# A two-layer decoder step on one core: the feed-forward input products of 18 of 22 column blocks as seven block products instead of eight

## The chip, the cores and the metric

The kernel runs on one core of a Trainium2 chip. The metric is the device time of one execution in microseconds (us). Engines are named as in the profile: PE is TensorE (its weight loads stand apart as PEld), DVE is VectorE, ACT is ScalarE, POOL is GpSimd, SP is SyncE, which here only issues transfers.

## The reference, cut to what matters

1,024 prompt tokens and 8 single new tokens go through two layers, an HGRN2 recurrence and a latent attention, each with a gated feed-forward behind it. Only the feed-forward is touched:

```
def swiglu(h, w_in, w_out):
    g, u = jnp.split(h @ w_in, 2, axis=-1)
    return (jax.nn.silu(g) * u) @ w_out
...
x = x + rmsnorm(mix, g[1])
x = x + rmsnorm(swiglu(rmsnorm(x, g[2]), w_ffn_in[l], w_ffn_out[l]), g[3])
```

The width is 1,024, w_in has 2 x 2,816 columns, and everything is float32.

## The kernel before, in words

All 1,032 tokens lie on the free axis, in three sets s of W = 344, and the model width is 8 chunks of 128 partitions. A float32 product is made of three fp32r products (`mm3`, lines 177 to 179): high weight by high x, high weight by low x, low weight by high x. `k.xh[s]` and `k.xl[s]` hold the high and the low half of x of a set, before the normalisation: the factor r[s] of the RMS norm is multiplied in after the product.

`ffn` walks the 2,816 hidden columns in 22 blocks f of 128. A block has a gate product and an up product for each set, each with 8 chunks of the width: 2 x 3 x 8 x 3 = 144 matmuls of 128 x 344. DVE multiplies the product by r[s] (L552, L556), ACT takes the silu (L553), POOL multiplies gate and up (L557), ACT and DVE split the result u into gh and gl (L129, L130), which stay in SBUF. One block behind follows the output product: 3 sets x 8 chunks x 3 = 72 matmuls of 128 x 344 (`out_chunk`), which DVE adds to acc (L582). The last three blocks' output products are made together, set by set, in the finishing stage (`outf`).

`k.weight` loads 512 KB of weights into a `raw` buffer (two of them, L148, on SP's queue), ACT casts the high half (L151), and POOL subtracts for the low half (L155). Weight tiles `w` have three buffers.

`finish` is what stands between two phases: for each set the sum of squares of the result (32-column matmuls of L252), its RMS norm, the residual x_d read back from DRAM, the new x, its two halves (L221, L222), and the squares of the new x (L252 again, or L198 for the last set, whose r is formed later). While the last set goes through this, PE has four products of the next phase to make, of the sets 0 and 1 (`first`).

The program is put in order per engine by a scheduler when it is built; an engine takes its instructions strictly in that order. PSUM has eight banks, all in one pool.

Of the kernel before, what the change touches and what calls it, by code (L numbers as in the profile page):

```python
# [23 lines left out]
NS = 3  # L24
W = T // NS
FF = 2816
# [11 lines left out]
class Core:  # L38
# [123 lines left out]
    def open_pre(self):  # L162

        self.pre, pool = self.right("pre", 2)
        return pool

    def close_pre(self):
        if self.pre is not None:
            self.pre.close()
            self.pre = None  # L170

    def mm3(self, out, terms, first=True, last=True):

        nc = self.nc
        n = len(terms)
        for i, ((wh, wl), (ah, al)) in enumerate(terms):
            nc.tensor.matmul(out, lhsT=wh, rhs=ah, start=first and i == 0, stop=False)  # L177
            nc.tensor.matmul(out, lhsT=wh, rhs=al, start=False, stop=False)  # L178
            nc.tensor.matmul(out, lhsT=wl, rhs=ah, start=False, stop=last and i == n - 1)  # L179
# [116 lines left out]
def finish(k, pool, outf, acc, g_post, g_next, x_d, prefetch, at, kn):  # L296
    first, lags = kn['first'], kn['lags']

# [14 lines left out]
    def norm(s, sq):  # L313
        last = s == NS - 1
        for _ in range(lags[0]):
            yield
        r1 = yield from sq.rstd()
        s2 = Squares(k, pool, rev=kn['rev2'])
        ss = []
        for c in range(KC):  # L320
            y = acc[s][:, c, :]
            xs = pool.tile([P, W], F32, name="xs", tag="xs", bufs=6)
# [3 lines left out]
            k.put_x(s, c, y, g_next)  # L326
            if not last:
# [11 lines left out]
        if not last:  # L339
            for _ in range(lags[1]):  # L340
                yield
            rs[s] = yield from s2.rstd(k.new_r(s))
        else:
            rs[s] = lambda pool, tags: result(k.rstd(pool, ss, k.one, D, k.new_r(s), tags))
# [9 lines left out]
    for s in range(NS):  # L354
        for i, sq in enumerate(products(s)):
            if s == at and i == 0:
                prefetch()
            catch_up(kn['rate'] if i else kn['rate0'])
        behind.append(norm(s, sq))
    for i, m in enumerate(first):  # L360
# [163 lines left out]
LAST = 3  # L524


def ffn_first(w_in):

    w_in = w_in.rearrange("(c p) f -> p c f", p=P)
    return [(w_in[:, :, :P], KC, P), (w_in[:, :, FF:FF + P], KC, P)]  # L530


def ffn(k, w_in, w_out, r, end):
    nc, tc = k.nc, k.tc
    w_in = w_in.rearrange("(c p) f -> p c f", p=P)
    with ExitStack() as st:
        accp = st.enter_context(tc.tile_pool(name="accp", bufs=1, reuse_waits="tile"))
        acc = [k.new_acc() if k.accs is not None and s < NS - 1 else accp.tile([P, KC, W], F32, name=f"acc{s}") for s in range(NS)]
        gp = st.enter_context(tc.tile_pool(name="gp", bufs=2, reuse_waits="tile"))
        G = {}  # L540
        wo = {}

        def inp(f):

            wg = k.weight(w_in[:, :, f * P:(f + 1) * P], KC, P)
            wu = k.weight(w_in[:, :, FF + f * P:FF + (f + 1) * P], KC, P)
            for s in range(NS):
                if callable(r[s]):
                    r[s] = r[s](gp, ("u", "a", "u"))
                pg = k.xproduct(wg, s, 0)  # L550
                a = gp.tile([P, W], F32, name="a")
                nc.vector.tensor_tensor(out=a, in0=pg, in1=r[s], op=ALU.mult)  # L552
                nc.scalar.activation(out=a, in_=a, func=AF.Silu)  # L553
                pu = k.xproduct(wu, s, 1)
                u = gp.tile([P, W], F32, name="u")
                nc.vector.tensor_tensor(out=u, in0=pu, in1=r[s], op=ALU.mult)  # L556
                nc.gpsimd.tensor_tensor(out=u, in0=u, in1=a, op=ALU.mult)  # L557
                gh = gp.tile([P, W], F32R, name="gh", bufs=NS * LAST + 1)
                gl = gp.tile([P, W], F32R, name="gl", bufs=NS * LAST + 1)
                k.split(gh, gl, u)  # L560
                G[f, s] = (gh, gl)
                if s == 0:
                    wo[f] = k.weight(w_out[f * P:(f + 1) * P, :].unsqueeze(1), 1, D, None, gp if f < NF - 1 else None)
                yield

        units = [inp(f) for f in range(NF)]
        for f, n in ((0, NS - 1), (1, NS - 1), (0, 1)):
            for _ in range(n):
                next(units[f])
        for f in range(1, NF):  # L570
            if f < NF - 1:
                for _ in units[f]:
                    pass
            k.close_pre()
            if f <= NF - LAST:
                for s in range(NS):
                    for dc in range(KC):
                        po = out_chunk(k, wo, G, [f - 1], s, dc)
                        if f == 1:
                            nc.scalar.copy(acc[s][:, dc, :], po)  # L580
                        else:
                            nc.vector.tensor_tensor(out=acc[s][:, dc, :], in0=po, in1=acc[s][:, dc, :], op=ALU.add)  # L582

        def outf(s, dc):
            if dc == 0:
                next(units[NF - 1])
# [1190 lines left out]
def tile_yoco_step(ctx, tc, a, c, o, phases=("hgrn", "ffn0", "mla", "ffn1")):  # L1777
# [16 lines left out]
    firsts = {  # L1794
        "hgrn": lambda: hgrn_first(a["w_in_a"][0]),
        "ffn0": lambda: ffn_first(a["w_ffn_in"][0]),
        "mla": lambda: mla_first(a, cols[:, 64:72]),
        "ffn1": lambda: ffn_first(a["w_ffn_in"][1]),
    }
    k.prefetch(firsts[phases[0]]())  # L1800
    load = lambda *tiles: load_x(k, a["x_prompt"], a["x_sample"], pre[phases[0]], x_d, *tiles)
    if phases[0] != "hgrn":
        with tc.tile_pool(name="ld", bufs=2, reuse_waits="tile") as lp:
            r = [g() for g in load(lambda: lp.tile([P, D], F32, name="xt"), lambda: lp.tile([P, KC, W], F32, name="y0"), lp)]
    for n, ph in enumerate(phases):
# [4 lines left out]
        def end(st, outf, acc):  # L1810
            prefetch, at = None, 1
            if ph in ("hgrn", "mla") and nxt is not None:
                prefetch = lambda: k.prefetch(firsts[nxt](), k.open_pre())
# [5 lines left out]
            return finish(k, fp, outf, acc, gain(l, gi + 1), pre[nxt], x_d, prefetch, at, KN[ph])  # L1819
# [19 lines left out]
        else:  # L1839
            r = ffn(k, a["w_ffn_in"][l], a["w_ffn_out"][l], r, end)  # L1840
# [69 lines left out]
```

## Time and profile before

| | |
|---|---|
| time, median of 3 runs | 2927.92 us (2924.86 to 2930.66) |
| profiled execution | 2927.77 us, span 2926.0 us, mean granted TensorE clock 0.977 |
| PE busy, share of the span | 2790.2 us, 95% |
| DVE, ACT, POOL busy | 1718.8, 1129.5, 999.3 us |
| moved by DMA | 242.51 MB, mean 83 GB/s |

The HGRN2 phase takes the first 640 us or so, the first feed-forward lies at about 750 to 1550 us, the attention up to about 2150 us, and the second feed-forward after that. [...]

### The profile page before, as it was taken

The page shows a single profiled execution, that of the slowest core. Times are in us where ns is not written, and L with a number is a line of the kernel's source. Part 1 is how long each engine was busy: PE and PEld are TensorE (multiplying, and loading weights), DVE is VectorE, ACT ScalarE, POOL GpSimd, SP SyncE. Part 2 cuts the span into 40 slices and gives each one's busy share as a digit, 9 for nine tenths or more (in the row PEclk, how much of TensorE's full clock was granted, in tenths as well). Part 3 has the DMA queues.
Part 4 walks back from the last instruction along what each step waited for, and adds up shares of the span by engine and source line. Part 5 has one row for each costly group of instructions (what it writes and reads, how often), then busy time and mean ns, then how long its engine had stood idle before and what let it go on. Part 6 is the DMA issues. An engine that isn't in the chain of part 4 may idle for free.

```text
span 2926.0 us, 54566 instructions
## 1 busy us (share of the span) xinstructions
PE 2790.2 (95%) x22360; PEld 2623.6 (90%) x22360; DVE 1718.8 (59%) x3298; ACT 1129.5 (39%) x2422; POOL 999.3 (34%) x912
## 2 busy tenths in 40 slices
PE   7998988889999999999999999979999999999998
PEld 7988888878899999999978899846889999999998
DVE  7888888863444444444358888794363444444435
ACT  7666666655511111111255766523453111111112
POOL 3555555552432233332332111242153332223320
PEclk9999999989999999999999999989999999999999
DMA  5122222152311111111132112486431111111112
GB/s 184 54 67 67 67 67 65 60 191 99 117 48 50 44 44 51 46 49 51 37 100 83 46 48 69 169 346 223 133 107 51 47 48 51 44 44 49 46 61 92
DMA packets 230970, 242.51 MB, mean 83 GB/s; under 512 B 19074, under 2 KB 211120, under 8 KB 224704
## 3 DMA queue, kind: packets, MB, share of 16 engines
q1 hardware_dynamic: 205456, 170.14, 19.0%
q0 software_dynamic: 7456, 43.00, 4.0%
q10 hardware_dynamic: 17808, 25.89, 2.5%
q8 instruction: 176, 2.88, 0.4%
q14 instruction: 74, 0.61, 0.1%
HBM read 194.87 MB, written 44.12 MB: 82 GB/s over the span
## 4 chain that ended last, share of the span: by engine, by line
PE 83%; DVE 9%; ACT 4%; issue 2%; DMA 1%; POOL 1%; SPq 0%; DVEq 0%; ACTq 0%; POOLq 0%
PE ps L177 24%; PE ps L178 24%; PE ps L179 23%; PE ps L252 2%; DVE E L873 1%; DVE turned L1458 1%; PE ps L1385 1%; PE ps L1458 1%; DVE X L877 1%; PE ps L903 1%; PE ps L940 1%; ACT E L875 1%; DVE X L1008 1%; PE ps L198 1%; DVE oy L1010 1%
## 5 line engine op out<-in xcount | busy, mean ns | idle before, releaser
L177 PE MATMUL ps<-xh,w 128*128 128x344 f32 x3360 | 1103.8, 329 | 1.9 <-ACT xh L221 1.9
L178 PE MATMUL ps<-xl,w 128*128 128x344 f32 x3360 | 1083.5, 323 | 1.6 <-DVE xl L222 1.6
L179 PE MATMUL ps<-xh,w 128*128 128x344 f32 x3360 | 1078.7, 322 | 0.0
L155 POOL TENSOR_TENSOR w<-raw,w 128x512 fp32r<-128x512 f32 (+1 forms) x360 | 466.3, 1316 | 809.5 <-ACT w L151 803.0
L177 PEld LDWEIGHTS ps<-xh,w 128*128 128x128 f32 x3360 | 638.6, 190 | 24.7 <-issue 12.1
L178 PEld LDWEIGHTS ps<-xl,w 128*128 128x128 f32 x3360 | 638.5, 190 | 15.3 <-issue 8.3
L179 PEld LDWEIGHTS ps<-xh,w 128*128 128x128 f32 x3360 | 637.5, 190 | 5.7 <-issue 5.6
L582 DVE TENSOR_TENSOR acc<-ps,acc 128x344 f32<-128x344 f32 x864 | 397.4, 513 | 0.0
L151 ACT CAST w<-raw 128x1024 fp32r<-128x1024 f32 (+4 forms) x206 | 206.5, 1004 | 423.7 <-PE ps L179 324.0
L177 PE MATMUL ps<-gh,w 128*128 128x344 f32 x1056 | 338.6, 323 | 0.5 <-ACT gh L129 0.3
L179 PE MATMUL ps<-gh,w 128*128 128x344 f32 x1056 | 338.5, 321 | 0.0
L178 PE MATMUL ps<-gl,w 128*128 128x344 f32 x1056 | 338.0, 320 | 0.0
L557 POOL TENSOR_TENSOR u<-u,a 128x344 f32<-128x344 f32 x132 | 122.1, 926 | 533.6 <-DVE u L556 529.0
L556 DVE TENSOR_TENSOR u<-ps,r 128x344 f32<-128x344 f32 x132 | 68.1, 516 | 388.6 <-PE ps L179 388.4
L129 ACT CAST gh<-u 128x344 fp32r<-128x344 f32 x132 | 63.5, 481 | 504.3 <-POOL u L557 504.3
L552 DVE TENSOR_TENSOR a<-ps,r 128x344 f32<-128x344 f32 x132 | 68.1, 516 | 231.6 <-PE ps L179 225.5
L177 PEld LDWEIGHTS ps<-gh,w 128*128 128x128 f32 x1056 | 198.2, 188 | 5.3 <-issue 1.7
L179 PEld LDWEIGHTS ps<-gh,w 128*128 128x128 f32 x1056 | 198.6, 188 | 1.1 <-issue 1.1
L178 PEld LDWEIGHTS ps<-gl,w 128*128 128x128 f32 x1056 | 198.6, 188 | 1.1 <-DVE gl L130 0.8
L130 DVE TENSOR_TENSOR gl<-u,gh 128x344 fp32r<-128x344 f32 x132 | 70.1, 531 | 150.9 <-ACT gh L129 150.9
L553 ACT ACTIVATE a<-a 128x344 f32<-128x344 f32 x132 | 64.5, 490 | 224.0 <-DVE a L552 223.8
L876 POOL TENSOR_TENSOR X<-lin,E 128x256 f32<-128x256 f32 x112 | 115.8, 1040 | 88.9 <-ACT E L875 32.4
(375 smaller groups left out, 4047.0 us busy)
## 6 DMA issues: line engine op xcount, KB each, us to landing
raw<-in_w_ffn_in_dram SPq DMA_DIRECT2D x88, 512.0 KB
raw<-in_w_ffn_out_dram SPq DMA_DIRECT2D x44, 512.0 KB
raw<-in_w_in_a_dram SPq DMA_DIRECT2D x32, 512.0 KB
xs<-x_d SPq DMA_DIRECT2D x72, 172.0 KB
x_d<-acc ACTq DMA_DIRECT2D x9, 1376.0 KB
x_d<-y SPq DMA_DIRECT2D x3, 1376.0 KB
od_a<-oh ACTq DMA_DIRECT2D x24, 172.0 KB
od_a<-ol ACTq DMA_DIRECT2D x24, 172.0 KB
```

The costliest lines, as they stand in the source:

```text
L130: (lo_eng or self.nc.vector).tensor_tensor(out=lo, in0=src, in1=hi, op=ALU.subtract)
L151: nc.scalar.copy(wh[:, :n], raw[:, :n])
L155: eng.tensor_tensor(out=wl[:, sl], in0=raw[:, sl], in1=wh[:, sl], op=ALU.subtract)
L177: nc.tensor.matmul(out, lhsT=wh, rhs=ah, start=first and i == 0, stop=False)
L178: nc.tensor.matmul(out, lhsT=wh, rhs=al, start=False, stop=False)
L179: nc.tensor.matmul(out, lhsT=wl, rhs=ah, start=False, stop=last and i == n - 1)
L552: nc.vector.tensor_tensor(out=a, in0=pg, in1=r[s], op=ALU.mult)
L553: nc.scalar.activation(out=a, in_=a, func=AF.Silu)
L556: nc.vector.tensor_tensor(out=u, in0=pu, in1=r[s], op=ALU.mult)
L557: nc.gpsimd.tensor_tensor(out=u, in0=u, in1=a, op=ALU.mult)
L582: nc.vector.tensor_tensor(out=acc[s][:, dc, :], in0=po, in1=acc[s][:, dc, :], op=ALU.add)
L876: nc.gpsimd.tensor_tensor(out=Xl[:, :, 0, :], in0=kl[:, :, 0, :], in1=El[:, :, 0, :], op=ALU.mult)
```

## The change: what it does

Both feed-forwards are rebuilt.

- **x normalised.** `finish` with `gated` forms r for all three sets, multiplies the new x by its gain and by r, and splits that (8 more DVE products, ACT copies and subtractions a set). The squares of set 2 go through the 32-column matmuls as well (L256 now). The buffers `xs` go from 6 to 4.
- **Plain blocks.** Blocks 0 to 3 stay 144 matmuls of 344 columns (`plain`). Blocks 0 and 1 of the sets 0 and 1 are made inside `finish` (`before`): eight products instead of four.
- **Seven products.** For blocks 4 to 21 gate and up are seen as a 2 x 2 block product: rows gate and up, inner halves of the width, columns two sets of tokens. The 1,032 tokens are four sets of Q = 258 (the fourth is gathered from the three ends of 86), taken as two pairs. Each pair needs seven products of 4 chunks (`PRODUCTS`), with combined weights S1 to S4 (`make`: POOL forms them, ACT and DVE split them, seven parts of 128 x 512 a block) and combined tokens T1 to T4 (`tokens`, `last_tokens`, once per layer). A block is then 2 x 7 x 4 x 3 = 168 matmuls of 128 x 258 (`visit`), and the sums are taken by accumulating further products on the same PSUM bank and by ACT and DVE outside it.
- **Through DRAM.** The split silu(g) u of each block is stored to `g_d` and read back (1,032 KB a block) in a separate output stage: block 0 alone, then nine pairs, then the last three in `outf` as before.

```
+Q = T // 4
+R = W - Q
...
 def finish(...):
+            if not gated:
+                k.put_x(s, c, y, g_next)
+            if not last or gated:
                 s2.add(acc[s][:, c:c + 1, :], None, xs)
...
+            r = rs[s] = yield from s2.rstd(k.new_r(s))
+            for c in range(KC if gated else 0):
+                xs = pool.tile([P, W], F32, name="xs", tag="xs", bufs=4)
+                nc.vector.scalar_tensor_tensor(out=xs, in0=acc[s][:, c, :], scalar=g_next[:, c:c + 1], in1=r, op0=ALU.mult, op1=ALU.mult)
+                k.split(k.xh[s][:, c, :], k.xl[s][:, c, :], xs, nc.gpsimd if last and c % 2 else None)
...
+    if gated:
+        for _ in gated.before():
+            catch_up(3)
...
+PRODUCTS = (("A11", "B11"), ("S1", "T1"), ("S2", "T2"), ("S4", "B22"), ("S3", "T3"), ("A12", "B21"), ("A22", "T4"))
...
+    def make(self, f):
+        A = []
+        for i in range(2):
+            raw = k.wp.tile([P, 1024], F32, name="raw", tag="raw", bufs=2)
+            nc.sync.dma_start(out=raw.rearrange("p (a b) -> p a b", a=KC), in_=self.columns(f, i))
+            A += [raw[:, :512], raw[:, 512:]]
+        src = dict(zip(("A11", "A12", "A21", "A22"), A))
+        how = {"S1": ("A21", "A22", ALU.add), "S2": ("S1", "A11", ALU.subtract), "S4": ("A12", "S2", ALU.subtract), "S3": ("A11", "A21", ALU.subtract)}
+        for name, _ in PRODUCTS:
+            if name in how:
...
+                nc.gpsimd.tensor_tensor(out=src[name], in0=src[a], in1=src[b], op=op)
+            w = self.slot()
+            hi, lo = w[:, :512], w[:, 512:1024]
+            k.split(hi, lo, src[name])
...
+    def visit(self, f):
...
+        for name, xname in PRODUCTS:
+            wh, wl = self.parts.pop((f, name))
+            for p in range(2):
+                xh, xl = self.X[p, xname]
...
+                k.mm3(to, [((wh[:, j, :], wl[:, j, :]), (xh[:, j, :], xl[:, j, :])) for j in range(KH)], not more, True, more)
+                if name == "A11":
+                    nc.scalar.copy(t1[p], to)
+                elif name == "S1":
+                    nc.scalar.copy(t5[p], to)
+                elif name == "S2":
+                    nc.scalar.copy(t2[p], to)
+                elif name == "S4":
+                    nc.vector.tensor_tensor(out=t2[p], in0=to, in1=t2[p], op=ALU.add)
+                    nc.scalar.activation(out=t2[p], in_=t2[p], func=AF.Silu)
+                elif name == "S3":
+                    nc.vector.tensor_tensor(out=t5[p], in0=to, in1=t5[p], op=ALU.add)
+                    nc.gpsimd.tensor_tensor(out=t5[p], in0=t5[p], in1=t2[p], op=ALU.mult)
+                    store(2 * p + 1, self.pool.tile([P, 2, Q], F32R, name="gs", tag="td"[p]), t5[p])
+                elif name == "A12":
+                    nc.vector.tensor_tensor(out=t1[p], in0=to, in1=t1[p], op=ALU.add)
+                    nc.scalar.activation(out=t1[p], in_=t1[p], func=AF.Silu)
+                else:
+                    nc.vector.tensor_tensor(out=t1[p], in0=to, in1=t1[p], op=ALU.mult)
...
 def ffn(...):
+    def fetch(f, new, pool=None):
+            t = new([P, 2, T])
+            nc.sync.dma_start(out=t.bitcast(F32), in_=g_d[f])
...
+            wo[f] = k.weight(w_out[f * P:(f + 1) * P, :].unsqueeze(1), 1, D, None, pool)
...
+        while f < NF - LAST:
+            fs = range(f, min(f + (GROUP if f else 1), NF - LAST))
+            for s in range(NS):
+                for dc in range(KC):
+                    n = fs[-1] + 1 + s
+                    if dc == 0 and s < 2 and n < NF:
+                        fetch(n, lambda shape: gp.tile(shape, F32R, name="G", bufs=4), gp if n % 2 else None)
+                    po = out_chunk(k, wo, G, fs, s, dc)
+                    if f == 0:
+                        nc.scalar.copy(acc[s][:, dc, :], po)
+                    else:
+                        nc.vector.tensor_tensor(out=acc[s][:, dc, :], in0=po, in1=acc[s][:, dc, :], op=ALU.add)
```

Three places of the built order follow, each before the change and after it where both have one.

On ACT, in the middle of a feed-forward, with the buffers' numbers: `w` are weight halves being cast, `a` and `gh` the gate and the split result. Before:

```order
L151 CAST w_11837<-raw_11836 128x1024
L151 CAST w_11591<-raw_11590 128x1024
L553 ACTIVATE a_11555<-a_11555 128x344
L129 CAST gh_11586<-u_11583 128x344
L553 ACTIVATE a_11621<-a_11621 128x344
L129 CAST gh_11652<-u_11649 128x344
L151 CAST w_11843<-raw_11842 128x1024
```

After, from the second product of a visit to its fifth (`t5` and `t2` are temporaries of the pairs 0 and 1, `S` the combined weights, `gs` the split result):

```order
L724 COPY t50_10487<-ps_10474 128x258
L724 COPY t51_10502<-ps_10489 128x258
L727 COPY t20_10518<-ps_10441 128x258
L727 COPY t21_10532<-ps_10456 128x258
L131 CAST w_10538<-raw_10534 128x512
L131 CAST w_10538<-S_10569 128x512
L730 ACTIVATE t20_10518<-t20_10518 128x258
L730 ACTIVATE t21_10532<-t21_10532 128x258
L131 CAST gs_10587<-t50_10487 128x258
L131 CAST w_10613<-S_10611 128x512
L131 CAST w_10613<-S_10646 128x512
```

ACT now empties PSUM, casts parts for the next block, and issues the stores, all in one line; a cast that waits for a transfer or for POOL stands ahead of the silus.

On ACT, where the first layer's last visit ends and the output stage begins (`acc` are the sums of the output product), after the change; the place is new:

```order
L131 CAST gs<-t_13919 128x258
L703 DMA g_d<-gs 256x1x258
L131 CAST gs<-t_13934 128x258
L703 DMA g_d<-gs 256x1x258
L153 CAST w<-raw 128x1024
L809 COPY acc_14144<-ps 128x344 x8
L153 CAST w<-raw 128x1024
L809 COPY acc_14145<-ps 128x344 x8
```

The first cast of w writes where gs lay (it waits for the store of the row above it), and the eight copies that free the PSUM banks stand behind it.

On SP's queue, in the second feed-forward: `xs<-x_d` are the three residuals for the kernel's last stage. Before, they stand behind all weights:

```order
L148 DMA raw<-in_w_ffn_in_dram 128x8x128 x2
L148 DMA raw<-in_w_ffn_out_dram 128x1024
L512 DMA xs<-x_d 128x2752 x3
L502 DMA out_dram<-yt 128x1024 x2
L502 DMA out_dram<-yt 88x1024
```

After:

```order
L616 DMA raw<-in_w_ffn_in_dram 128x8x128 x36
L150 DMA raw<-in_w_ffn_out_dram 128x1024 x3
L527 DMA xs<-x_d 128x2752 x3
L150 DMA raw<-in_w_ffn_out_dram 128x1024
L475 DMA g_row<-in_norm_gains_dram 128x1024
L785 DMA G<-g_d 128x2064 x4
L150 DMA raw<-in_w_ffn_out_dram 128x1024 x4
```

They moved to the end of the visits, where x is no longer needed, and ahead of the first reads of g_d.

## Rows read from the trace of the kernel before

**Rows 1.** The page: busy time and share of engines; PE in 40 slices; the chain.

```profile
PE 2790.2 (95%) x22360; PEld 2623.6 (90%) x22360; DVE 1718.8 (59%) x3298; ACT 1129.5 (39%) x2422; POOL 999.3 (34%) x912
...
PE   7998988889999999999999999979999999999998
...
PE ps L177 24%; PE ps L178 24%; PE ps L179 23%; PE ps L252 2%; DVE E L873 1%; DVE turned L1458 1%; PE ps L1385 1%; PE ps L1458 1%; DVE X L877 1%; PE ps L903 1%; PE ps L940 1%; ACT E L875 1%; DVE X L1008 1%; PE ps L198 1%; DVE oy L1010 1%
```

**Rows 2.** Windows: length, busy (instructions) of PE, PEld, DVE, ACT, POOL; clock, DMA, GB/s.

```profile
1000.00:1050.00 50.00, 50.00 (x321) 50.00 (x320) 25.07 (x55) 8.56 (x12) 15.47 (x13) 1.00 0.19 53
1050.00:1100.00 50.00, 50.00 (x320) 50.00 (x319) 19.62 (x43) 8.85 (x14) 15.64 (x14) 1.00 0.11 34
```

**Rows 3.** Timeline of PE: 24 matmuls of 256 columns lie between the two rows.

```profile
1619.05 0.28 PE L177 MATMUL ps<-w,ch 128*128 128x256 f32 x1
...
1621.89 0.28 PE L177 MATMUL ps<-w,ch 128*128 128x256 f32 x1
```

**Rows 4.** By tile, ch: duration min/median/max; first and last start; the same matmuls.

```profile
L177 PEld LDWEIGHTS ps<-w,ch x64: 187/188/191, 1618.9 to 1828.9; 128*128 128x128 f32 x64
```

**Rows 5.** Windows at the entries of the two feed-forwards, columns as in 2.

```profile
760.00:770.00 10.00, 7.62 (x49) 7.33 (x47) 10.00 (x11) 6.36 (x13) 9.10 (x8) 1.00 0.35 144
770.00:780.00 10.00, 5.91 (x20) 5.00 (x21) 7.09 (x14) 5.59 (x9) 6.11 (x6) 0.66 0.34 98
...
2160.00:2170.00 10.00, 9.77 (x63) 9.49 (x61) 10.00 (x11) 6.69 (x15) 8.64 (x8) 1.00 0.39 142
2170.00:2180.00 10.00, 3.70 (x9) 2.79 (x10) 7.42 (x12) 5.18 (x6) 5.99 (x5) 0.74 0.27 88
2180.00:2190.00 10.00, 10.00 (x61) 10.00 (x60) 4.31 (x8) 3.40 (x8) 6.18 (x8) 0.92 0.50 159
```

**Rows 6.** Timeline of PE around a 32-column reduction (L252), and at the entry wait.

```profile
1516.56 0.32 PE L178 MATMUL ps<-xl,w 128*128 128x344 f32 x1
1516.81 0.77 PE L252 MATMUL ps<-xs,one 128*32 128x344 f32 x2
1517.50 0.42 PE L179 MATMUL ps<-xh,w 128*128 128x344 f32 x1
1517.76 0.32 PE L177 MATMUL ps<-xh,w 128*128 128x344 f32 x1
...
774.09 2.63 PE L198 MATMUL ps<-ss,one 128*128 128x344 f32 x4 [6.48 <-DVE a L552]
```

**Rows 7.** By tile, raw: duration min/median/max of the weight cast and its subtractions.

```profile
L155 POOL TENSOR_TENSOR w<-raw,w x360: 726/1291/1800, 13.8 to 2842.6; 128x512 fp32r<-128x512 f32 x176, 128x256 fp32r<-128x256 f32 x4
L151 ACT CAST w<-raw x206: 405/1048/1292, 12.6 to 2839.8; 128x1024 fp32r<-128x1024 f32 x93, 128x256 fp32r<-128x256 f32 x4, 128x768 fp32r<-128x768 f32 x2, 128x512 fp32r<-128x512 f32 x2
...
L155 DVE TENSOR_TENSOR w<-raw,w x36: 417/684/2389, 651.0 to 2059.1; 128x512 fp32r<-128x512 f32 x28, 128x256 fp32r<-128x256 f32 x4, 128x384 fp32r<-128x384 f32 x4
```

**Rows 8.** By tile, u: the same columns, for 344 columns on POOL, ACT and DVE.

```profile
L557 POOL TENSOR_TENSOR u<-u,a x132: 921/925/938, 777.2 to 2895.8; 128x344 f32<-128x344 f32 x132
L129 ACT CAST gh<-u x132: 462/480/529, 778.1 to 2896.8; 128x344 fp32r<-128x344 f32 x132
L130 DVE TENSOR_TENSOR gl<-u,gh x132: 503/518/1077, 778.6 to 2897.3; 128x344 fp32r<-128x344 f32 x132
```

**Rows 9.** Timeline of one weight load: its issue on SP's queue, the cast that waited for it.

```profile
996.69 0.37 SPq L148 DMA_DIRECT2D raw<-in_w_ffn_in_dram  x1
...
1000.47 1.05 ACT L151 CAST w<-raw 128x1024 fp32r<-128x1024 f32 x1 [1.58 <-DMA raw<-in_w_ffn_in_dram]
```

**Rows 10.** Windows with a saturated DMA, and in the two finishing stages; columns as in 2.

```profile
660.00:670.00 10.00, 10.00 (x57) 7.05 (x56) 0.00 (x0) 3.19 (x7) 1.15 (x1) 1.00 1.00 337
1540.00:1550.00 10.00, 6.49 (x42) 6.21 (x41) 10.00 (x10) 5.67 (x15) 8.74 (x9) 1.00 0.59 199
2910.00:2920.00 10.00, 6.49 (x48) 5.41 (x46) 7.24 (x19) 3.13 (x13) 0.00 (x0) 0.95 0.06 23
```

**Rows 11.** The page's DMA issues: count, KB each.

```profile
raw<-in_w_ffn_in_dram SPq DMA_DIRECT2D x88, 512.0 KB
...
xs<-x_d SPq DMA_DIRECT2D x3, 1376.0 KB
```

More of the change, by code (lines that the diff above doesn't have):

```diff
@@ L162, in open_pre, with mm3 @@
     def open_pre(self):
-        self.pre, pool = self.right("pre", 2)
-        return pool
+        self.pre = self.right("pre", 2)
+        return self.pre[1]
     def close_pre(self):
         if self.pre is not None:
-            self.pre.close()
+            self.pre[0].close()
             self.pre = None
-    def mm3(self, out, terms, first=True, last=True):
+    def mm3(self, out, terms, first=True, last=True, more=False):
         nc = self.nc
         n = len(terms)
+        skip = {"skip_group_check": True} if more else {}
         for i, ((wh, wl), (ah, al)) in enumerate(terms):
-            nc.tensor.matmul(out, lhsT=wh, rhs=ah, start=first and i == 0, stop=False)
-            nc.tensor.matmul(out, lhsT=wh, rhs=al, start=False, stop=False)
-            nc.tensor.matmul(out, lhsT=wl, rhs=ah, start=False, stop=last and i == n - 1)
+            nc.tensor.matmul(out, lhsT=wh, rhs=ah, start=first and i == 0, stop=False, **skip)
+            nc.tensor.matmul(out, lhsT=wh, rhs=al, start=False, stop=False, **skip)
+            nc.tensor.matmul(out, lhsT=wl, rhs=ah, start=False, stop=last and i == n - 1, **skip)
     def xterm(self, k, s):
@@ L293, with finish @@
 }
-def finish(k, pool, outf, acc, g_post, g_next, x_d, prefetch, at, kn):
+def finish(k, pool, outf, acc, g_post, g_next, x_d, prefetch, at, kn, gated=None):
     first, lags = kn['first'], kn['lags']
@@ L357, in finish @@
                 prefetch()
-            catch_up(kn['rate'] if i else kn['rate0'])
+            catch_up(3 if gated else kn['rate'] if i else kn['rate0'])
         behind.append(norm(s, sq))
-    for i, m in enumerate(first):
+    if gated:
+        for _ in gated.before():
+            catch_up(3)
+    for i, m in enumerate(() if gated else first):
         n, s = divmod(i, NS - 1)
@@ new lines, in ffn, with then @@
+def ffn(k, gated, w_out, g_d, end):
+    nc, tc = k.nc, k.tc
+    G, wo = {}, {}
+    def fetch(f, new, pool=None):
+        if (f, 0) not in G:
+            t = new([P, 2, T])
+            nc.sync.dma_start(out=t.bitcast(F32), in_=g_d[f])
+            for s in range(NS):
+                G[f, s] = tuple(t[:, i, s * W:(s + 1) * W] for i in range(2))
+        if f not in wo:
+            wo[f] = k.weight(w_out[f * P:(f + 1) * P, :].unsqueeze(1), 1, D, None, pool)
+    def then():
+        fetch(0, lambda shape: k.pre[1].tile(shape, F32R, name="w", tag="w1", bufs=1))
+    gated.run(then)
@@ L536, in ffn @@
     with ExitStack() as st:
         accp = st.enter_context(tc.tile_pool(name="accp", bufs=1, reuse_waits="tile"))
+        gp = st.enter_context(tc.tile_pool(name="gp", bufs=2, reuse_waits="tile"))
         acc = [k.new_acc() if k.accs is not None and s < NS - 1 else accp.tile([P, KC, W], F32, name=f"acc{s}") for s in range(NS)]
[L539 to L546, printed above, removed]
-            for s in range(NS):
[L548 to L573, printed above, removed]
-            k.close_pre()
[L575 to L582, printed above, removed]
+        f = 0
@@ L584, in outf @@
+        for f in range(NF - LAST, NF):
+            fetch(f, lambda shape: gp.tile(shape, F32R, name="G", bufs=4), gp if f % 2 else None)
         def outf(s, dc):
-            if dc == 0:
-                next(units[NF - 1])
             po = out_chunk(k, wo, G, range(NF - LAST, NF), s, dc)
@@ L1839, in tile_yoco_step @@
         else:
-            r = ffn(k, a["w_ffn_in"][l], a["w_ffn_out"][l], r, end)
+            r = ffn(k, gated[ph], a["w_ffn_out"][l], g_d, end)
     k.close_x()
```

191 lines of the change are left out of this document (169 added, 22 removed).

## The prediction

> **What bounds the kernel now.** I read the page first, then stretches of the two feed-forwards, then single instructions. On the page PE is busy 95% of the span, no slice of it is under 7 tenths, and the chain that ended last runs for 71% through the three lines of the fp32r products [rows 1]. [...] What PE loses lies at the edges. At each entry it waits for x of the last set: 6.5 us of idleness in front of the last reduction [rows 6], and then matmuls at a granted clock below 1. In 760 to 780 us it makes 69 matmuls where 128 fit, in 2160 to 2190 us 133 where 192 fit [rows 5]: 59 x 0.156 = 9.2 us lost, twice.
>
> **The products.** A block of 144 matmuls costs 144 x 156.0 = 22.46 us. The pace of 258 columns isn't in the trace, but 256 is: 24 matmuls in 1621.89 - 1619.05 = 2.84 us, 118.3 ns each, with a weight load of its own for every matmul, as here [rows 3, 4]. From 256 and 344 a column costs (156.0 - 118.3) / 88 = 0.43 ns, so 258 columns cost 119.2 ns; about 0.5 ns either way changes little. A visit is 168 x 119.2 = 20.03 us, which saves 2.44 us a block, 87.8 us over 2 x 18 blocks. Blocks 0 to 3 and all output products keep their matmuls.
>
> That pace rests on loads being hidden. A weight load shows 187 to 191 ns even where matmuls start every 118 ns [rows 3, 4], so loads overlap matmuls and one another. [...]
>
> **Does anything else hold up a visit?** I price one visit on each engine. ACT: a cast is 0.480 us for 344 columns and 1.048 for 1,024 [rows 7, 8], so about 0.62 for 512 and 0.41 for 258. Seven parts and 14 PSUM copies, silus and splits make 10.1 us; six stores, at SP's 0.37 us for an issue [rows 9], another 2.2: 12.3 of 20.0. DVE: 0.68 us for 512 columns and 0.43 for 258, between its rows [rows 7, 8]; 7 and 12 of them make 9.9. POOL: four at 1.29 and two at no more than 0.93 make 7.0. None is full. The longest ring is a weight buffer's: load 3.8 us from issue to cast [rows 9], then S1, S2, S4, S3 on POOL one after another (5.2), seven casts (4.3) and a last subtraction (0.7): 14.0 us even if nothing overlaps. The parts are made some five products ahead (14 us), and a PSUM bank is read up to 4.3 us before it is written again. So steady visits cost me nothing extra; I take 3 us for the two first visits of the layers, where the token sums (about 31 us of DVE work) have 60 us of plain blocks to hide behind. Above I bound it by one subtraction of 0.68 us that PE waits for in every visit, 24 us; below, nothing.
>
> **The entries.** The eight plain products of `before` cover 30 us instead of 15. The chain of set 2 grows by a second reduction (about 4 us with its ACT and DVE steps), and by eight subtractions more on DVE (4 us): less than the 15 us of cover. Two reductions follow their own PSUM copy directly on PE, so I leave 2.5 us of wait at each entry (0 to 9.2, the row of before). Against that, each time PE turns to 32-column matmuls and back costs about 0.89 us however many stand together: from 1516.56 to 1517.76 is 1.20 us for two matmuls of 0.156 and one such turn [rows 6]. In the built order the first entry has 31 turns where it had 19, the second 17 where it had 18. Sum: - 18.4 + 12 x 0.9 - 0.9 + 5.0 = - 3.5 us (from - 9 to + 11).
>
> **From visits to output.** This place is new, and nothing hides what is late there. First layer: the first copies out of PSUM stand on ACT behind a cast that waits until the last store has landed. After the last matmul come the product on DVE, cast, subtraction (about 1.3 us), the store (2 to 3.8 us from issue, under the 512 KB load's [rows 9]), the cast (1.05) and a copy (0.45): some 6.0 us, while eight banks of 3 x 156 ns feed PE for 3.7. That is 2.3 us. Second layer: three residuals of 1,376 KB [rows 11] are now asked for some 4 us before the visits end, ahead of the reads of g_d. Until block 2's g_d has come, 4.23 MB of residuals, 1.05 of weights and gains, and 2 x 1.06 must pass: 7.4 MB, at the 337 GB/s of a saturated window [rows 10] 21.9 us, beginning about 3 us before the end. It is complete 19 us after it; PE has block 0 alone for 72 x 0.156 = 11.2 us and 0.5 us of block 1. So 7.2 us of wait, and 1.2 for matmuls at the lower clock, as after the entry's wait [rows 5]: 8.4. Together + 10.7 (2 to 14). Inside the output stage a pair of blocks takes 22.5 us and 3.2 MB, 140 GB/s: hidden.
>
> **The finishing stages.** The 22.5 us of block 21's input products stood inside each, as cover. Both already show windows where PE is busy 6.5 of 10 us, the first with DVE full [rows 10]. The first loses five turns (- 4.5 us); I take + 4.5 for the cover there and + 2 in the last stage (together - 3 to + 12).
>
> **Sum.** - 87.8 + 3.0 - 3.5 + 10.7 + 2.0 = - 75.6 us. The profiled execution took 2927.77 us, 0.15 below the median of 2927.92, with 1.8 us outside the span of 2926.0. So span 2850.4, time 2852.
>
> **Rivals.**
> - *Visits half spoiled.* A cast or a subtraction that waits for a weight load stands ahead of PSUM work in the strict order of ACT and DVE. If PE then loses half of what a visit saves, 1.2 us x 36 = 44: 2896. For it: the orders on ACT, where casts of the next block stand before the silus. Against it: the margins above.
> - *Slower: the ring of the weight buffers sets the visit.* If making the seven parts, with its waits for buffers, takes over 20.0 + 75.6 / 36 = 22.1 us, the gain is gone. At 24 us a visit it is + 143: 2995. Against it: 14.0 us by rows, and every engine under two thirds.
> - *The pace does not shrink.* If loads or issue held 258 columns at 156 ns, a visit would be 26.2 us: 36 x 3.75 = + 135 instead of - 88, so 3075. Rows 3 speak against it. [...]
> - *Edges free.* No wait at the entries (- 5.0), at the hand-over 2 instead of 10.7, nothing for first visits and finishing stages: 2852 - 18.7 = 2833.
>
> **How the numbers follow.** The forecast has a chance of 0.70, with its own range 2836 to 2872 from the bounds of entries, hand-over and finishing stages; edges free 0.08; half spoiled 0.13; the ring 0.07; the pace 0.02. Reaching down to 2832 and up to 2885 takes in the forecast, edges free and part of half spoiled, and leaves out about 2 in 10. A change within 0.2% (6 us) is about what a measurement here can't tell from none: only a ring or a loss near 22.1 us a visit gives it, 0.03. Slower: the rest of the ring and the pace, 0.06. Faster: 0.91. Predicted: 2852 us.
>
> **What would show it.** In windows inside the visits: PE full and some 419 matmuls in 50 us, spaced 119 ns; DVE near half, ACT near 60%. At the entries: under 3 us of wait, and turns to 32-column matmuls. At the second hand-over: a wait of PE for G from g_d of some 7 us, with xs<-x_d under way; at the first, about 2 us on ACT's copy of acc. Wrong would be the forecast if PE shows idle time in every visit (released by ACT or DVE), if the 258-column matmuls start more than 122 ns apart, or if the granted clock falls between visits.

## The result and the profile after

The kernel after takes 2960.02 us (median of 4 runs, 2957.67 to 2963.19) beside 2928.02 for the one before (4 runs): ratio 1.011, 95% interval 1.0093 to 1.0128. It is slower by 32 us where 76 us less were forecast. The profiled execution has a span of 2961.4 us, 35.4 longer than before. In some sets of runs one step of the attention stage, which the change does not touch, takes 146 to 151 us instead of 134 to 140, and the kernel before some 2940 us instead of 2928, so below every ratio is to the kernel before in the same set.

The page after, for [rows 1]: PE's busy time falls by 48 us, yet its share falls too, and a transfer stands in the chain, with a subtraction on DVE and POOL's sums.

```profile
PE 2741.9 (93%) x23252; PEld 2551.6 (86%) x23252; DVE 1854.7 (63%) x3348; ACT 1291.2 (44%) x2936; POOL 981.2 (33%) x894
...
PE ps L181 14%; PE ps L182 14%; PE ps L183 13%; DMA raw<-in_w_ffn_in_dram 5%; DVE w L132 3%; POOL S L624 2%; PE ps L1689 2%; ACT w L131 2%; PE ps L256 1%; DVE t L659 1%; DVE E L1104 1%; ACTq L706 1%; DVE gs L132 1%; PE ps L1616 1%; DVE X L1108 1%
```

By stages, from the starts of matmuls (an entry runs from the last matmul of the stage before the feed-forward to the first visit, and is set against the same number of 344-column matmuls before the change; times in us, differences rounded on their own):

| stage | before | after | difference | forecast |
|---|---|---|---|---|
| entries, layers 1 and 2 | 209.7, 205.0 | 219.9, 212.7 | + 17.9 | - 3.5 |
| visits, and the 18 blocks in their place | 407.0, 407.2 | 399.2, 400.3 | - 14.8 | - 84.8 |
| hand-over, output and finish | 361.9, 278.2 | 380.7, 292.7 | + 33.2 | + 12.7 |
| the rest | | | - 0.9 | 0 |

The visits miss their forecast by 70 us, the other two by some 21 each. What a visit loses stands in PE's waits, here inside the visits of layer 1 (total us, times, longest):

```profile
PE ps L181 <- ACT t L721: 18.9, 17, 4.7
PE ps L181 <- DVE t L732: 4.7, 7, 2.0
PE ps L181 <- ACT t L727: 0.4, 1, 0.4
```

L721 is ACT's copy of the first product out of PSUM, which the third product of the same bank waits for: once in almost every visit. In the two layers, 66 matmuls of 258 columns start over 260 ns behind the one before, which costs 60.7 us more than 119.2 ns each; 138 that start after 160 to 260 ns, most of them behind such waits, cost 13.4; all others stand 119.9 ns apart (4 us). That is the 78 us between 36 visits at 20.03 us and the 799.5 measured.

What stood ahead of the copy, ACT's timeline in one visit (start, length, idle time before it; ACTq is an issue), and PE's matmul that waited:

```profile
1006.36 0.41 ACT L131 CAST gs<-t 128x258 fp32r<-128x258 f32 x1 [0.55 <-DVE t L739]
1006.69 1.86 ACTq L706 DMA_DIRECT2D g_d<-gs  x3
1008.59 0.63 ACTq L703 DMA_DIRECT2D g_d<-gs  x1
1009.27 0.41 ACT L131 CAST gs<-t 128x258 fp32r<-128x258 f32 x1 [2.50 <-issue]
1009.58 0.37 ACT L721 COPY t<-ps 128x258 f32<-128x258 f32 x1
...
1010.00 0.39 PE L181 MATMUL ps<-X,w 128*128 128x258 f32 x1 [0.85 <-ACT t L721]
```

Four issues of 0.62 us are ahead of the copy. And the chain that ended last, its pieces in order of time in the next visit (start, length), goes on for 23 us, from 1028.97 to 1052, without one matmul:

```profile
1029.19 0.40 ACT gs L131
1029.61 0.43 DVE gs L132
...
1031.95 0.52 ACTq L703
1032.51 0.38 ACT t L721
1032.88 0.56 ACT t L724 x2
1033.44 0.52 ACT w L131
1033.98 0.70 DVE w L132
1034.70 5.68 DMA raw<-in_w_ffn_in_dram
1040.55 1.26 POOL S L624
1041.83 0.63 ACT w L131
1042.49 1.24 DVE w L132
1043.86 1.28 POOL S L624
1045.14 1.15 POOL t L733
1046.32 0.42 ACT gs L131
...
1048.41 0.63 ACT w L131
1049.07 0.56 DVE w L132
...
1051.62 0.64 ACTq L706
```

It is a ring: the last cast and subtraction of a block's weights free the buffer, the load of the next block takes 5.7 us, its sums, casts and subtractions follow, between them the gate, the splits and the stores of the block in work, and then the last casts again.

### The profile page after: what moved, and what is told of

Same layout as the page of the kernel before. It is cut to its first block, busy times and chain, and to the rows that moved or that the text cites. A ratio compares the mean times of both kernels' runs of the same rounds, so it can differ in the third digit from the quotient of the medians.

```text
span 2961.4 us, 57997 instructions
## 1 busy us (share of the span) xinstructions
PE 2741.9 (93%) x23252; PEld 2551.6 (86%) x23252; DVE 1854.7 (63%) x3348; ACT 1291.2 (44%) x2936; POOL 981.2 (33%) x894
## 4 chain that ended last, share of the span: by engine, by line
PE 53%; DVE 17%; ACT 9%; DMA 8%; issue 7%; POOL 4%; ACTq 2%; DVEq 0%; POOLq 0%; SPq 0%
PE ps L181 14%; PE ps L182 14%; PE ps L183 13%; DMA raw<-in_w_ffn_in_dram 5%; DVE w L132 3%; POOL S L624 2%; PE ps L1689 2%; ACT w L131 2%; PE ps L256 1%; DVE t L659 1%; DVE E L1104 1%; ACTq L706 1%; DVE gs L132 1%; PE ps L1616 1%; DVE X L1108 1%
## 5 line engine op out<-in xcount | busy, mean ns | idle before, releaser
L181 PE MATMUL ps<-xh,w 128*128 128x344 f32 (+1 forms) x2496 | 793.9, 319 | 11.3 <-DVE t L732 8.0
L182 PE MATMUL ps<-xl,w 128*128 128x344 f32 (+1 forms) x2496 | 775.2, 311 | 2.8 <-DVE xl L226 1.6
L183 PE MATMUL ps<-xh,w 128*128 128x344 f32 (+1 forms) x2496 | 769.7, 309 | 0.0
L157 POOL TENSOR_TENSOR w<-raw,w 128x512 fp32r<-128x512 f32 (+1 forms) x216 | 287.0, 1349 | 738.8 <-ACT w L153 720.8
L181 PEld LDWEIGHTS ps<-xh,w 128*128 128x128 f32 x2496 | 475.9, 191 | 36.0 <-issue 12.6
L182 PEld LDWEIGHTS ps<-xl,w 128*128 128x128 f32 x2496 | 476.4, 191 | 16.1 <-issue 6.7
L183 PEld LDWEIGHTS ps<-xh,w 128*128 128x128 f32 x2496 | 476.1, 191 | 6.3 <-issue 6.1
L811 DVE TENSOR_TENSOR acc<-ps,acc 128x344 f32<-128x344 f32 x432 | 222.8, 517 | 220.9 <-PE ps L183 220.5
L181 PE MATMUL ps<-G,w 128*128 128x344 f32 x1008 | 326.4, 324 | 3.9 <-DMA G<-g_d 3.3
L182 PE MATMUL ps<-G,w 128*128 128x344 f32 x1008 | 325.2, 323 | 0.0
L183 PE MATMUL ps<-G,w 128*128 128x344 f32 x1008 | 324.0, 321 | 0.5 <-POOL w L157 0.5
L181 PE MATMUL ps<-X,w 128*128 128x258 f32 x720 | 209.8, 291 | 21.1 <-ACT t L721 18.9
L132 DVE TENSOR_TENSOR w<-S,w 128x512 fp32r<-128x512 f32 x144 | 155.6, 1091 | 109.9 <-ACT w L131 109.8
L182 PE MATMUL ps<-X,w 128*128 128x258 f32 x720 | 204.3, 284 | 0.0
L183 PE MATMUL ps<-X,w 128*128 128x258 f32 x720 | 203.9, 283 | 0.0
L181 PEld LDWEIGHTS ps<-G,w 128*128 128x128 f32 x1008 | 190.9, 189 | 9.0 <-issue 6.3
L183 PEld LDWEIGHTS ps<-G,w 128*128 128x128 f32 x1008 | 191.1, 190 | 1.9 <-issue 1.1
L182 PEld LDWEIGHTS ps<-G,w 128*128 128x128 f32 x1008 | 190.7, 189 | 2.0 <-issue 1.7
L181 PEld LDWEIGHTS ps<-X,w 128*128 128x128 f32 x720 | 137.7, 191 | 27.9 <-ACT t L721 22.5
```

The lines of the kernel that those rows point to most:

```text
L132: (lo_eng or self.nc.vector).tensor_tensor(out=lo, in0=src, in1=hi, op=ALU.subtract)
L157: eng.tensor_tensor(out=wl[:, sl], in0=raw[:, sl], in1=wh[:, sl], op=ALU.subtract)
```

## The experiments

Three theories stood at the start. A: the six stores on ACT delay the copies. B: the loads into two buffers come late, and casts and subtractions that wait for them hold ACT and DVE up. C: the visits are as good as they can be and the round trip through DRAM loses. Ratios are to the kernel before, run beside each; ratios and stages are compared, not times. "A visit" is the mean over 18 with the first one (22.18 and 22.24 us in the two layers of the kernel after).

**Stores from SP.** `nc.scalar.dma_start` becomes `nc.sync.dma_start` in both places of `store`.

> The change as it is, but the stores of the visits' products are issued by SP instead of ACT. Theory A (the six stores, which stand in ACT's strict order ahead of the copies out of PSUM and take 0.52 to 0.64 us each there, make PE wait in every visit): the 39 us of PE's waits for ACT's copy t of the visits go, a visit falls from 22.2 to about 20.6 us, and at the first hand-over the last store is ahead of the reads of g_d, so that wait falls from 15.5 to about 4 us: some 2900 us. Theory B (the loads of the input weights into two buffers come late, and the casts and subtractions that wait for them hold ACT and DVE up): the visits stay at 22 us, only the hand-over gains: some 2949 us.

Ratio 0.9903 (0.9886 to 0.9919); a visit 20.71 and 20.68 us. From visits to the finish 7.6 us less in layer 1; PE's wait there is still 7.0 us.

**A third buffer for loaded weights**, in `make`:

```
-raw = k.wp.tile([P, 1024], F32, name="raw", tag="raw", bufs=2)
+raw = self.pool.tile([P, 1024], F32, name="raw2") if (2 * f + i) % 3 == 2 else k.wp.tile([P, 1024], F32, name="raw", tag="raw", bufs=2)
```

> The change as it is, but with a third buffer for the input weights as loaded, used in turn, so that a block's weights are asked for before the last parts of the block before are made. Theory A (stores in ACT's order): POOL's idle stretch of 13 us a visit shrinks, but PE still waits for ACT's copy in every visit: 2945 to 2960 us. Theory B (late weights): a visit falls to about 20.6 us and the time to some 2905 us.

Ratio 0.9881 (0.9864 to 0.9897); a visit 20.49 and 20.45 us. B's numbers; but with the stores on SP, A's had come true as well.

**One store for three pieces.**

```
-for s in range(NS):
-    nc.scalar.dma_start(out=to[:, :, s * W + Q:(s + 1) * W], in_=v[:, :, s * R:(s + 1) * R])
+nc.scalar.dma_start(out=to.rearrange("p i (s w) -> p i s w", w=W)[:, :, :, Q:], in_=v.rearrange("p i (s r) -> p i s r", r=R))
```

> The change as it is, but the three pieces of the fourth set go out in one store with one more dimension, so that ACT issues four stores a visit instead of six. Theory A: 1.2 us of ACT less in front of the copies, of a wait of 1.7 us a visit: a gain of 20 to 40 us, some 2930 us. Theory B: no change beyond 5 us, 2955 to 2965 us.

Ratio 0.9918 (0.9902 to 0.9935); a visit 20.79 and 20.67 us: more than the 1.2 us of the two issues. The loads still come late here (ACT waits 21 us in 200 for them, as before this edit), and PE does not mind.

**All blocks plain:** `PLAIN, AHEAD = 22, 2`, and no sums of tokens.

> All 22 blocks by plain products, none by block products, and no sums of tokens; x kept normalised, the round trip of silu(g) u through DRAM and the output stage in pairs stay. By the stages of the two traces the visits save only 15 us against plain blocks, and the rest of the change costs 50: without them the time is some 2975 us, less what the sums of tokens cost at the entries (up to 10 us a layer): 2955 to 2975. The rival, that the visits themselves are what loses and the round trip is free: 2930 us, as before the change.

Ratio 1.0077 (1.0058 to 1.0096): the rest of the change costs 0.8%, and the visits, as they ran, made the whole 0.3% slower still (1.011), which is hardly clear of the noise. The blocks themselves are not the reason: 18 plain ones take 406.1 us in each layer, where the visits take 399.2 and 400.3. But behind them PE waits at neither hand-over here, and the time from the blocks to the finish is 17 and 11 us shorter than after the change. Set against the kernel before, these last stages, with the round trip through DRAM, cost only some 5 us here, and the entries 17.8. So C is wrong on both counts: the visits were not as good as they can be, and the round trip by itself costs little.

**Third buffer and stores from SP; third buffer and one store.** The edits above, together.

> The change with both the third buffer for loaded weights and the stores on SP. Theory R (a ring sets the visit: weight load, POOL's sums, casts, gate, stores and copies one behind another in the strict orders of ACT, DVE and POOL; each of the three changes so far makes it shorter than PE's products): a visit that was 20.5 and 20.7 us with one of them is 20.2 to 20.5 with both, so the ratio to the kernel before is 0.983 to 0.988. Theory S (two separate costs that add, 60 and 67 us): PE's own products would have to be overtaken, so nearer 0.975.

> The change with the third buffer and one store for the fourth set instead of three. Theory R: as with stores on SP, a visit of 20.2 to 20.5 us; ratio 0.984 to 0.988. Theory S: 0.976.

Ratios 0.9857 (0.984 to 0.9874) and 0.9872 (0.9856 to 0.9889). A visit is 20.45 to 20.51 us in all four layers, as with the third buffer alone: nothing adds, so PE itself is the limit there. What SP's stores still bring stands at the first hand-over (365.0 us from there to the finish, against 374.5 with one store on ACT).

**The hand-over mended**, on top of the third buffer and the one store: block 1's output weights in another pool, and a one-column copy that the load of the residual has to wait for.

```
-fetch(n, lambda shape: gp.tile(shape, F32R, name="G", bufs=4), gp if n % 2 else None)
+fetch(n, lambda shape: gp.tile(shape, F32R, name="G", bufs=4), gp if n % 2 and n > 1 else None)
...
+nc.vector.tensor_copy(xs[:, 0, :1], acc[s][:, KC - 1, :1])
 nc.sync.dma_start(out=xs, in_=x_d[s])
```

> As the kernel with the third buffer and the one store, and at the hand-over to the output stage block 1's output weights go to a buffer that no store of the visits holds, and the residuals are asked for only when the last blocks' products are reached. If the waits there are the store's landing behind the reads of g_d (first layer, 7 to 15 us) and the residuals ahead of these reads (second layer, 6 to 10 us), each falls to under 3 us: 10 to 16 us less than without, ratio about 0.980. The rival, that the reads of g_d themselves are what PE waits for: no more than 3 us less.

Ratio 0.9823 (0.9807 to 0.984), 0.5% less. From the visits to the finish 364.4 and 282.3 us instead of 374.5 and 287.7. What stood there after the change, ACT's timeline at the first hand-over:

```profile
1249.34 0.52 ACTq L703 DMA_DIRECT2D g_d<-gs  x1
1263.03 1.04 ACT L153 CAST w<-raw 128x1024 fp32r<-128x1024 f32 x1 [14.18 <-DMA g_d<-gs]
1263.98 2.88 ACT L809 COPY acc<-ps 128x344 f32<-128x344 f32 x8
```

and what stands there with the mend (PE's only wait at this place is now 0.7 us, for g_d):

```profile
1215.55 0.52 ACTq L704 DMA_DIRECT2D g_d<-gs  x1
1216.11 2.89 ACT L809 COPY acc<-ps 128x344 f32<-128x344 f32 x8 [1.93 <-PE ps L183]
1218.82 1.13 ACT L153 CAST w<-raw 128x1024 fp32r<-128x1024 f32 x1
```

**The last sum of tokens in the first visit**, by its place in the code.

```
-for _ in itertools.chain(forming, *(self.last_tokens(p) for p in range(2))):
+for _ in forming:
     pass
+late = itertools.chain(*(self.last_tokens(p) for p in range(2)))
...
 next(steps)
+next(late, None)
```

> As the kernel with the mended hand-over, and the last sum of tokens (T4, for the seventh product) is formed during the first visit instead of ahead of it. If PE's wait of 4 to 5 us in each first visit is DVE's queue of token sums ahead of ACT's copy, it falls to about 1 us: 6 to 8 us less, ratio about 0.978. The rival, that the plain blocks' last store or the weights hold the copy: no change.

Ratio 0.9833 (0.9817 to 0.985), and the same wait of 4.4 us. It tells nothing of the cause: the built program has the instructions of every engine in the same order as the kernel with the mended hand-over, so this is a second run of that. The cause stays argued from the trace: ACT's copy stands there behind the split of the last plain block's result, which waits for DVE, full with sums of tokens (busy 8.9 of the 10 us from 850 on in this run).

**The suspected cost doubled:** six pieces for three (`to[:, i, ...]` for both halves), with two buffers and with three.

> The change with the suspected cost doubled: the fourth set's store goes out in six pieces instead of three, the same bytes, so that ACT has nine issues a visit. Theory R (the ring that runs through ACT's issues, with two buffers for loaded weights, sets the visit): three more issues of 0.62 us lengthen the visit from 22.2 to about 24 us; ratio about 1.034. The rival, that the late loads alone set the visit and ACT has slack: 1.011 to 1.014.

> The same six pieces, with the third buffer for loaded weights. Theory R: with the third buffer the ring is no longer closed within a visit and what ACT has more to do is hidden: a visit of 20.5 to 20.8 us, ratio 0.988 to 0.995. The rival, that issues on ACT delay the copies for PE whatever the loads do: 1.9 us a visit more than with three pieces, ratio about 1.011.

Ratios 1.0072 (1.0055 to 1.0089) and 0.9911 (0.9895 to 0.9928). With two buffers a visit is 21.89 and 21.75 us: shorter than with three pieces, though the six issues take 3.05 us in a row instead of 1.86. Theory R, by the time that issues take, missed, and so did the rival's 1.011. The order had changed with it: in one visit of the trace, for example, a cast of loaded weights now starts ahead of each of the last two stores. With three buffers, 20.49 and 20.46 us, as R had it.

**The same six issues elsewhere.** Two buffers; the fourth set's stores and those of the last product are kept in a list and issued later, ordered on ACT behind an instruction: first behind the next visit's two copies L721, then behind the cast of the next visit's last weight part, the one that frees the second buffer.

```
+copied = nc.scalar.copy(t1[p], to)
+if p:
+    with k.tc.issue_after(copied.ins):
+        stores()
...
+cast = k.split(hi, lo, src[name])
+if name == "A22":
+    with k.tc.issue_after(cast.ins):
+        self.stores()
```

> The change with two buffers and all six stores still issued by ACT, but the stores of the fourth set and of the last product of a visit are held, by an order on ACT alone, behind the next visit's copies of its first product out of PSUM; nothing else is changed. If the place of the stores ahead of these copies is what makes PE wait (as six pieces in place of three, elsewhere in the order, cost nothing more), a visit falls from 22.2 to 20.6 to 20.9 us, as with stores on SP: ratio 0.990 to 0.993. If it is the time that ACT spends on six issues, wherever they stand, the visit stays above 21.5 us: ratio 1.005 or more.

> As the kernel with the stores held back, but behind the cast of the block's last weight part (the one that frees the second buffer of loaded weights) instead of the copies alone, so that the same six issues on ACT no longer stand between the end of a visit and the next load. Theory R, made sharper (a visit is as long as the round from one load of the weights to the next, and an issue on ACT costs where it stands in that round): the next loads start earlier, a visit falls to 20.6 to 21.0 us, ratio 0.990 to 0.995. The rival, that ACT's time on issues counts wherever it stands: the visit stays above 21.8 us, ratio 1.006 or more.

Ratios 1.0185 (1.0168 to 1.0203) and 0.9947 (0.993 to 0.9963); a visit 22.38 and 22.50 us, and 20.77 and 20.94. Behind the copies, nothing was gained: the place ahead of the copies L721 alone is not the cause. ACT's timeline of that run has the issues ahead of the weight casts, and SP's queue the next loads behind them:

```profile
1009.64 3.37 ACTq L710 DMA_DIRECT2D g_d<-gs  x5
1013.06 0.62 ACT L131 CAST w<-raw 128x512 fp32r<-128x512 f32 x1 [3.06 <-issue]
...
1014.47 1.12 SPq L616 DMA_DIRECT2D raw<-in_w_ffn_in_dram  x2
```

This run does not clear the issues of holding up copies, for they now stand ahead of the next ones (L732 there). PE's waits in 300 us:

```profile
PE ps L181 <- ACT t L732: 9.8, 7, 1.9
PE ps L181 <- DVE t L740: 8.5, 14, 2.4
```

Behind the last cast, the casts run with the issues, the loads go out, and the last two stores follow:

```profile
1037.35 0.52 ACTq L698 DMA_DIRECT2D g_d<-gs  x1
1037.55 0.62 ACT L131 CAST w<-raw 128x512 fp32r<-128x512 f32 x1
1037.90 0.64 ACTq L698 DMA_DIRECT2D g_d<-gs  x1
1038.08 0.63 ACT L131 CAST w<-raw 128x512 fp32r<-128x512 f32 x1
...
1038.97 1.15 SPq L617 DMA_DIRECT2D raw<-in_w_ffn_in_dram  x2
```

The issues still stand beside those next copies (L733 there), and PE hardly waits for them, again in 300 us:

```profile
PE ps L182 <- DVE t L741: 2.2, 4, 1.3
PE ps L182 <- ACT t L733: 0.8, 1, 0.8
```

So with two buffers an issue costs by where it stands in the round from load to load. One stretch of steady visits, by windows (the first number in brackets is PE's matmuls in 200 us), in the kernel after:

```profile
950.00:1150.00 200.00, 188.93 (x1529) 185.65 (x1528) 97.00 (x173) 78.20 (x189) 62.07 (x54) 0.99 0.34 98
```

With the stores behind the copies:

```profile
950.00:1150.00 200.00, 188.39 (x1518) 184.19 (x1517) 101.22 (x169) 78.30 (x187) 65.95 (x54) 0.99 0.34 96
```

With the stores behind the last cast:

```profile
950.00:1150.00 200.00, 197.85 (x1641) 197.01 (x1640) 107.83 (x184) 86.58 (x205) 70.90 (x56) 1.00 0.38 106
```

With the third buffer, stores as in the change:

```profile
950.00:1150.00 200.00, 200.00 (x1670) 200.00 (x1669) 101.63 (x190) 86.56 (x208) 69.21 (x60) 1.00 0.37 105
```

At 168 matmuls a visit that is 22.0, 22.1, 20.5 and 20.1 us; the forecast was 20.03.

**The entries:** five buffers xs instead of four (they were six before the change), and `catch_up(4)` for `catch_up(3)`, each on the kernel with the mended hand-over.

> As the kernel with the mended hand-over, with five buffers xs instead of four in the finishing of x at the entries. If PE's waits for the squares (11 us in all, in front of the 32-column sums) come from the buffers that the change took from six to four, they fall by a third: 3 to 4 us less, ratio about 0.981. The rival, that the squares wait for the reduction ahead of them: no change, 0.982 to 0.983.

> As the kernel with the mended hand-over, with four steps of the finishing of x between products instead of three, which leaves 56 groups of 32-column matmuls in the program instead of 68. If the entries lose by the turns, 12 of 0.8 us go: some 10 us less, ratio about 0.979. The rival, that sums asked for earlier wait longer for their squares: the waits take back what the turns give, 0.982.

Ratios 0.9823 (0.9807 to 0.984) and 0.9883 (0.9867 to 0.99). Five buffers: the entries take 219.6 and 209.8 us against 218.2 and 214.9, no difference in the whole. The second entry may still gain: with five buffers it takes 209.8 here and 210.1 in the run below, with four 211.2 to 217.8 in the other runs of three steps between products. Fewer turns: the entries are 4.1 and 10.4 us longer. The groups of 32-column matmuls fall from 31 to 21 and from 16 to 14, but their cost, from the starts around each, only from 26.6 to 25.4 and from 18.1 to 17.7 us (0.86 and 1.13 us a group became 1.21 and 1.26), and PE's waits at them double, from 5.1 to 9.6 and from 9.6 to 19.8. The rival came true, and more: it gave 0.982.

**All mends together:** third buffer, stores from SP, both mends of the hand-over, five buffers xs.

> The mends together: third buffer for loaded weights, stores on SP, the hand-over's two mends, five buffers xs. If what each takes away is no longer on the path once the visits are held by PE alone, it is within 0.3% of the kernel with the mended hand-over, ratio 0.980 to 0.983. The rival, that stores on SP and the mended hand-over still add up there: 0.976 to 0.979.

Ratio 0.9807 (0.979 to 0.9823), 2872.72 us beside 2928.5: 1.9% less than the kernel before and the fastest version, though its interval overlaps that of the kernel with the mended hand-over alone (0.9823).

## Why the prediction was wrong, point by point

- *The products* held. The 156.0 ns of a matmul of 344 columns, on which they rest, are 100 us over the 641 matmuls of [rows 2]. Matmuls of 258 columns show 0.28 us each, but their starts stand 119.9 ns apart with a weight load each; 119.2 were forecast, at a granted clock of 1.00 but for three stretches of 3 to 7 us at 0.5, behind starts that lie 2.3, 5.0 and 5.1 us apart. With a third buffer PE is busy for 200.00 of 200 us.
- *Does anything else hold up a visit?* **This is the step that failed**, by 70 of the 111 us between the forecast span and the measured one. It concluded "steady visits cost me nothing extra" from busy times under two thirds and a ring of 14.0 us. The rival *the ring of the weight buffers sets the visit*, by which the gain is gone from 22.1 us on, had 7 in 100; the visits took 22.2 in the mean, 21.9 without the first of each layer. The pricing had four faults. The ring of 14.0 us took the load at 3.8 us, where the chain has 5.7 to the first sum. It took 0.68 us for the subtraction of a part: for those made from sums the mean is 1.09 (in the group of the page below; 0.69 for parts taken as loaded). The 72 of them that run while POOL works take 1.49 in the mean, the other 72 0.69. Why, the traces do not show. ACT's 12.3 us priced a store's issue at 0.37 us, where it is 0.52 alone and 0.62 in a row: six make 3.5 us a visit, not 2.2. And, the largest (the other three come nowhere near 22 us), the ring counted the parts alone, "even if nothing overlaps", though gates, splits, copies and stores stand among them in one line on each engine. That the line is strict the trace shows: ACT's copy L721 at 1009.58 stands behind four issues, from 1006.69 to 1009.22, and 3,339 of DVE's 3,348 instructions start, by their lines, in the built order. I had named that strictness for the rival *half spoiled* and given it no price in the ring. The two groups of the page after, mean and idle time behind the bar:

```profile
L132 DVE TENSOR_TENSOR w<-S,w 128x512 fp32r<-128x512 f32 x144 | 155.6, 1091 | 109.9 <-ACT w L131 109.8
...
L132 DVE TENSOR_TENSOR w<-raw,w 128x512 fp32r<-128x512 f32 x108 | 73.0, 690 | 156.8 <-ACT w L131 145.4
```

- What is shown: with a third buffer the visit is PE's however the stores are issued (one, three or six pieces on ACT, or on SP: 20.35 to 20.51 us with the first visit in it, 20.1 to 20.3 for every later one); with two, the same six issues give 22.4 and 22.5 us ahead of the casts that free the buffers and 20.8 and 20.9 beside and behind them. What is not: how the 1.5 us that one store for three gains divide between two issues less and the order that changed with them. The scheduler sets the order anew for each kernel: by the traces, leaving the issues of transfers out, 36 (one store) to 212 (behind the last cast) of ACT's 2,900 instructions stand elsewhere than in the kernel after, so no run here changes one thing alone.
- *First visits:* 1.5 us each were forecast, but one wait for L721 alone took 4.7 and 4.8. The first visits last 26.6 and 27.1 us, and still 26.2 and 26.4 with the third buffer; they are part of the 70 us.
- *The entries* cost 17.9 instead of giving 3.5 us. The term of the turns was near: the groups of 32-column matmuls cost 14.1 us more (forecast 9.9). The term "- 18.4", the waits of before taken off, failed, and with it the 5.0 left for waits: all idle time of PE in the two entries is 6.1 and 12.3 us where it was 7.0 and 6.5. The one long wait became several of up to 3 us, for squares and reductions; PE's waits at the second entry:

```profile
PE ps L256 <- ACT xs L245: 5.3, 3, 2.5
PE ps L202 <- ACT rs_m L264: 3.7, 5, 1.4
```

- *From visits to output,* layer 1: right in kind, 2.3 us forecast, 15.5 measured. The store's "2 to 3.8 us from issue" is the wrong term. The store was issued at 1249.34, and the cast behind its landing began at 1263.03; four reads of g_d (4 x 1,032 KB or 4.23 MB, 12.5 us at the 337 GB/s of [rows 10], 10.8 at the 392 of the 5 us from 1250 on and 10.0 at the 423 of the next 5) had been issued from 1247.9 on. With the stores from SP, issued ahead of these reads, the same cast begins at 1226.82, 6.9 us behind the issue of the last two stores, and PE waits 7.0 us instead of 15.5: by these two traces the reads ahead of the store cost about half, and a store ahead of them takes longer than forecast too. Layer 2: 8.4 forecast, as a wait on g_d; 7.1 came, on the copies of acc, which stand behind a cast that waited for a store's landing while the three residuals were under way:

```profile
2678.20 0.41 ACT L131 CAST gs<-t 128x258 fp32r<-128x258 f32 x1 [8.25 <-DMA g_d<-gs]
```

  PE's one wait on g_d in this layer, 3.3 us, comes 230 us later. Behind the two waits the matmuls of 344 columns start 0.287 us apart, at a granted clock of 0.5, against 0.158 at 1.00 right behind, which costs another 2.5 and 1.9 us. With both mends the two stages from the visits to the end are 10.1 and 5.4 us shorter, so the store's landing and the residuals were on the path.
- *Finishing stages* are in the third row of the table. 27 of its 33 us are the hand-overs' waits and the low clock behind them; the run with all blocks plain, which has neither, is some 5 us above the kernel before in these stages, where 2.0 were forecast.

## What to carry to other kernels

When a tuned loop gets its work spread over four engines, do not judge it by busy shares: follow one buffer round, from its load to its next load, through every instruction that stands in line with its users, and compare that round with the bound engine's time; here no engine but PE was over two thirds busy (DVE 63% of the span) and the round still set the pace. Here one more buffer opened the ring however the stores in it were issued (a visit of 20.35 to 20.51 us instead of 22.2); it is the first thing to try. At a hand-over between stages, look for a small store that lands behind large reads, and for memory that only its landing frees (here ACT stood 14.2 us for it).

## What the runs showed of the hardware that was not expected

- The issue of a store cost by the piece here, not by its bytes: alone 0.52 us for 258 KB and for 86 KB alike, 0.63 to 0.64 right behind another; so 258 KB took 0.52 us in one piece, 1.86 in three, about 3 in six (2.75 to 3.28). On SP three took 1.84 us and one 0.53, while a weight load's issue alone took 0.37 there: the difference went with the transfer, not with the queue.
- Behind a wait, mostly of about 1 us, the first matmul of 258 columns took some 0.22 us until the next one started, and not 0.12, though the granted clock was 1.00 (62 of 66 waits). Of the 138 slow starts, 47 stand in the three stretches granted 0.5, 0.21 to 0.22 us apart.
